# One decoder layer in fp32 on one core: a bias table stored in 16 copies instead of 128, S5 outputs grouped by four state tiles, and two activation tiles at other SBUF offsets

## The chip, the core and the metric

The kernel runs on one core of a Trainium2 chip. The metric is the device time in microseconds of one execution. A core has five engines that run beside each other: TensorE (PE; its weight loads, PEld, overlap its matmuls), VectorE (DVE), ScalarE (ACT), GpSimd (POOL) and SyncE (SP). Each has an instruction stream of its own, run in order; 16 DMA engines serve the transfers that the engines' queues issue. The profile gives TensorE's granted clock as a share: 1.00 is 2.4 GHz, 0.50 is 1.2 GHz.

## The reference

One decoder layer over 256 tokens of width 2048, all in float32: a token mixer, a cross attention into 256 memory tokens and a gated MLP, each followed by a residual and a layer norm. The mixer has three groups behind one input projection: an S5 state space group (512 channels, 32 groups of 16 channels with 64 complex states each), 8 stick-breaking attention heads and 16 NSA heads. What matters here, in the reference's words:

```python
# S5 group: per 16-channel group a diagonal complex recurrence, then the outputs from its states
xr_in = jnp.einsum('btgc,gpc->btgp', ug, br)
xi_in = jnp.einsum('btgc,gpc->btgp', ug, bi)
_, _, sr, si = lax.associative_scan(_complex_affine, (a_r, a_i, xr_in, xi_in), axis=1)
y = jnp.einsum('btgp,gcp->btgc', sr, c_re) - jnp.einsum('btgp,gcp->btgc', si, c_im)
y = y.reshape(bsz, t_len, S5_CH) + d * uf
...
# NSA: a T5 relative-position bias (32 buckets x 16 heads) is added to the logits;
# it depends on the distance t - s of query and key alone
```

## The kernel before

The program walks once through the layer. Every weight matrix comes in chunks of 128x1024 float32 (512 KB). SyncE's queue loads a chunk into `raw` (4 buffers), ScalarE copies it rounded to `hi` (L277, 3 buffers), VectorE subtracts the rest, `lo = raw - hi` (L278, 3 buffers), and TensorE makes three matmuls of every 128x128 piece: hi by hi, hi by lo, lo by hi. Two helpers do this. In `mm3` (L292 to L294) the weights are stationary and the activations move, 256 columns at a time, 24 matmuls a chunk; it serves the mixer's input projection with `A` as moving operand, and the up-projection of the MLP, w_up, with the four tiles `mix` as moving operand (`mix0` and `mix1` for the first half of the contraction, `mix2` and `mix3` for the second). In `mm3x` (L300 to L302) the activations are stationary and the weights move, up to 512 columns at a time; it serves the output projections, among them that of the MLP, w_down, whose activations lie in `A` (re-used) and `act`.

The S5 group runs beside the mixer's projections: `s5_work` is a Python generator from which each weight chunk takes some steps, so its instructions stand between those of the projections. It first builds two tables `Ec` and `Es` [128, 16 state tiles, 256 tokens] (cosines and sines of the rotation), then for each state tile s takes the inputs (two matmuls into `pb`), turns them by the table, scans, and turns back into `s5z`. `outputs(s, ...)` multiplies `s5z` by the matrix `cmat` (in listings `s5c`): two matmuls of 32 columns into column quarter s modulo 4 of a PSUM tile `pa`, the real part and the imaginary one, and after each fourth state tile a VectorE instruction that ends the group. The profile gives these matmuls the line of a small helper, L182, which only orders an S5 instruction behind a projection's. A matmul with float32 operands leaves two records in the trace.

The NSA bias is made by `nsa_bias`, early in the mixer: one small matmul gives `g_sb`, 384 values for each of 16 heads, in 16 SBUF partitions. GpSimd's queue writes it to a DRAM tile `g_dr`, 128 copies of each head's row. In `nsa`, after the queries, ScalarE's queue reads it back into `slab` [128 partitions, 16 heads, 256] through a skewed access pattern with a step of 383 where a copy has 384 values: partition p reads copy p one value further back, which turns the bias by distance into a bias by query and key. Four transfers bring four heads each, 1 KB for each partition and head. VectorE reads `slab` first in L992 and L994 (bias added to a head's logits, and the minimum taken); exponentials, sums and the transposes of L1018 on TensorE follow, head by head. Ahead of them stand the eight tiles of queries, `nq`: ScalarE L940 and VectorE L941 take each from its projection.

The order of the instructions on each engine is fixed when the kernel is built, by a scheduler that simulates the program with priorities by lane; at run time each engine follows it and waits on semaphores. TensorE's stream therefore has projections, S5 matmuls and attention matmuls interleaved as that scheduler put them. Pools decide where tiles lie in SBUF.

Of the kernel before, what the change touches and what calls it, by code (L numbers as in the profile page):

```python
# [8 lines left out]
F32 = mybir.dt.float32  # L9
F32R = mybir.dt.float32r  # L10
ACTF = mybir.ActivationFunctionType
ALU = mybir.AluOpType
# [21 lines left out]
LN2_LO = math.log(2.0) - LN2_HI  # L34
RES_COLS = ((0, 512), (512, 512), (1024, 512), (1536, 256), (1792, 256))
CST_AT = 3
NORM0, NORM1, HOLD = 3, (2,), 2
TABLE_PACE, SCAN_PACE = 0.8, 2.8
BUCKET_FROM = [16, 21, 27, 35, 46, 59, 77, 99, 128, 166, 216]
# [150 lines left out]
class Program:  # L190
    def __init__(self, tc, a, out, ctx):
        self.tc, self.nc, self.a, self.out, self.ctx = tc, tc.nc, a, out, ctx
        pool = lambda name, bufs, **kw: ctx.enter_context(tc.tile_pool(name=name, bufs=bufs, **kw))
        self.lanes = {"first": 0, "split": 100_000, "mixer": 200_000, "proj": 300_000,
                      "late": 400_000}
        self.cur_lane, self.turns = "mixer", False
        self.holds = []
        self.background, self.pace, self.credit = None, 0.0, 0.0
        self.last_hi = self.last_lo = self.last_mm = None
        self.mm_marks = [None, None, None]  # L200
        self.bv = Behind(self, self.nc.vector, lambda: self.last_lo)
        self.bs = Behind(self, self.nc.scalar, lambda: self.last_hi)
        self.bt = Behind(self, self.nc.tensor, lambda: self.mm_marks[-2])
        tc.cur_priority = self.lanes["mixer"]
        self.consts = pool("consts", 1)
        self.wraw = pool("wraw", 4)
        self.whi = pool("whi", 3)
        self.wlo = pool("wlo", 3)
        self.acts = pool("acts", 1)
        self.stat = pool("stat", 2)  # L210
        self.pj = pool("pj", 3, space=bass.MemoryType.PSUM)
        self.op = pool("op", 1, space=bass.MemoryType.PSUM)
        self.mx = pool("mx", 2, space=bass.MemoryType.PSUM)
        self.pq = pool("pq", 1, space=bass.MemoryType.PSUM)
        self.dram = pool("dram", 1, space=bass.MemoryType.DRAM)

    @contextmanager
    def lane(self, name):
# [396 lines left out]
    def s5_work(self, cr, ci, f, fh, fl):  # L615
# [39 lines left out]
                         start=True, stop=True)  # L655
            return bu

        def outputs(s, sr):
            t, rows = s // 4, slice(32 * (s % 4), 32 * (s % 4) + 32)
            if s % 4 == 0:  # L660
                self.yps = self.pq.tile([128, 512], F32, name="pa")
            for i in range(2):
                T.matmul(self.yps[rows, :256], cmat[:, i, s, :], sr[:, i],
                         start=i == 0, stop=i == 1)
            if s % 4 == 3:
                V.scalar_tensor_tensor(self.s5y[:, t, :], u[:, t, :], self.s5d[:, t:t + 1],
                                       self.yps[:, :256], ALU.mult, ALU.add)

        bu, before = inputs(0), None
        yield 1  # L670
        for s in range(16):
            bu2 = bu.rearrange("p (i t) -> p i t", i=2)
# [7 lines left out]
            V.tensor_mul(m2, bu2, sb)  # L680
            if s < 15:
                bu = inputs(s + 1)
            if before is not None:
                outputs(s - 1, before)
            yield 1
            V.tensor_add(z[:, 0], m1[:, 0], m2[:, 1])
            V.tensor_sub(z[:, 1], m1[:, 1], m2[:, 0])
# [5 lines left out]
            V.tensor_mul(m3, z, cb)  # L693
            yield 1
            V.tensor_mul(m4, z, sb)
            before = w.tile([128, 2, 256], F32, name="s5z")
            V.tensor_sub(before[:, 0], m3[:, 0], m4[:, 1])
            V.scalar_tensor_tensor(before[:, 1], m3[:, 1], -1.0, m4[:, 0], ALU.mult, ALU.subtract)
            yield 1
        outputs(15, before)  # L700
        yield 1

    def s5_inputs(self, cr, ci):
# [116 lines left out]
    def nsa_bias(self):  # L820
        nc, a, V, S = self.nc, self.a, self.nc.vector, self.nc.scalar
        both = self.nsq.tile([33, 2, 384], F32, name="oh", tag="kv")
        oh, g_sb = both[:, 0], both[0:NH, 1]
        tab = self.nsq.tile([33, NH], F32, name="tab")
        nc.scalar.dma_start(oh, a["oh"])
        V.memset(tab[32:33, :], -BIG)
        nc.scalar.dma_start(tab[0:32, :], a["relb"])
        g_ps = self.mx.tile([128, 512], F32, name="mx")
        nc.tensor.matmul(g_ps[0:NH, 0:384], tab, oh, start=True, stop=True)
        S.activation(g_sb, g_ps[0:NH, 0:384], ACTF.Copy, scale=-1.0)  # L830

        self.g_dr = self.dram.tile([NH, 128, 384], F32, name="g_dr")
        nc.gpsimd.dma_start(self.g_dr, g_sb.unsqueeze(1).to_broadcast([NH, 128, 384]))

    def nsa_compress(self):
        nc, a, V, S = self.nc, self.a, self.nc.vector, self.nc.scalar
# [109 lines left out]
    def nsa(self):  # L946
# [2 lines left out]
        vcb, vv, gate, ks, q = self.vcb, self.vv, self.gate, self.ks, self.nq  # L949
        g_dr = self.g_dr  # L950
        slab = p.tile([128, NH, 256], F32, name="slab")
        for c in range(4):
            src = bass.AP(g_dr.tensor, g_dr.offset + 127 + c * 4 * 128 * 384,
                          [[383, 128], [128 * 384, 4], [1, 256]])
            nc.scalar.dma_start(slab[:, 4 * c:4 * c + 4, :], src)
        self.after(S.activation(gate, gate, ACTF.Exp, scale=-1.0), self.table)
        V.tensor_scalar(gate, gate, 1.0, None, ALU.add)
        V.reciprocal(gate, gate)
# [285 lines left out]

    def ffn(self, H):
        nc, a, V, S = self.nc, self.a, self.nc.vector, self.nc.scalar
        p = self.ctx.enter_context(self.tc.tile_pool(name="ffp", bufs=1))
        w = self.ctx.enter_context(self.tc.tile_pool(name="ffw", bufs=2))
        cv = p.tile([128, NFF, 2, 4], F32, name="cv")
# [57 lines left out]
```

## Time and profile before

| | |
|---|---|
| device time, median of 3 runs | 1328.58 us (1328.31 to 1328.77) |
| the profiled execution, its own time | 1328.4 us |
| its span, first to last instruction | 1326.6 us |
| mean granted clock of TensorE | 0.989 |
| TensorE busy | 1288.9 us, 97% of the span |
| VectorE, ScalarE busy | 883.9 us (67%), 659.8 us (50%) |
| share of TensorE in the chain that ended last | 89% |

A busy time is the sum of an engine's instructions. The chain is followed back from the last instruction, at each step to what released it, so it tells whose work set the end.

### The profile page before, as it was taken

The page shows a single profiled execution, that of the slowest core. Times are in us where ns is not written, and L with a number is a line of the kernel's source. Part 1 is how long each engine was busy: PE and PEld are TensorE (multiplying, and loading weights), DVE is VectorE, ACT ScalarE, POOL GpSimd, SP SyncE. Part 2 cuts the span into 40 slices and gives each one's busy share as a digit, 9 for nine tenths or more (in the row PEclk, how much of TensorE's full clock was granted, in tenths as well). Part 3 has the DMA queues.
Part 4 walks back from the last instruction along what each step waited for, and adds up shares of the span by engine and source line. Part 5 has one row for each costly group of instructions (what it writes and reads, how often), then busy time and mean ns, then how long its engine had stood idle before and what let it go on. Part 6 is the DMA issues. An engine that isn't in the chain of part 4 may idle for free.

```text
span 1326.6 us, 23002 instructions
## 1 busy us (share of the span) xinstructions
PE 1288.9 (97%) x9221; PEld 1183.9 (89%) x9221; DVE 883.9 (67%) x1510; ACT 659.8 (50%) x1030; POOL 13.8 (1%) x23
## 2 busy tenths in 40 slices
PE   7978999999999999999999999999999999999996
PEld 7767788998779899889999999999999988888896
DVE  7757889787675585766666666666666654544457
ACT  6854333666564346355555555555555543333342
POOL 0200000000000000000000000000000000000000
PEclk9988999999999999989999999999999999999999
DMA  8694335563447555435656555555555665556573
GB/s 305 192 131 162 102 126 155 175 224 111 134 141 256 185 174 199 152 114 191 187 185 188 189 190 191 188 186 187 189 189 190 229 216 188 193 185 193 178 237 129
DMA packets 69414, 240.12 MB, mean 181 GB/s; under 512 B 7723, under 2 KB 10572, under 8 KB 68540
## 3 DMA queue, kind: packets, MB, share of 16 engines
q1 hardware_dynamic: 64720, 230.21, 53.0%
q0 software_dynamic: 1376, 4.98, 2.8%
q10 hardware_dynamic: 3212, 3.47, 0.8%
q8 instruction: 72, 1.18, 0.4%
q14 instruction: 34, 0.28, 0.1%
HBM read 231.82 MB, written 5.24 MB: 179 GB/s over the span
## 4 chain that ended last, share of the span: by engine, by line
PE 89%; DMA 4%; DVE 3%; ACT 2%; issue 1%; POOL 0%; ACTq 0%; DVEq 0%
PE pj L292 17%; PE pj L294 17%; PE pj L293 17%; PE pj L300 10%; PE pj L301 10%; PE pj L302 10%; DMA raw<-in_win_c 2%; PE pa L1025 2%; PE pa L182 1%; DMA s5us<-Ec 1%; DMA raw<-in_win_u 1%; ACT hi L277 1%; PE mx L858 1%; PE mx L988 1%; PE mx L989 1%
## 5 line engine op out<-in xcount | busy, mean ns | idle before, releaser
L278 DVE TENSOR_TENSOR lo<-raw,hi 128x1024 fp32r<-128x1024 f32 (+2 forms) x403 | 488.3, 1212 | 372.9 <-ACT hi L277 369.8
L277 ACT CAST hi<-raw 128x1024 fp32r<-128x1024 f32 (+2 forms) x403 | 419.3, 1040 | 532.5 <-PE pj L293 286.7
L292 PE MATMUL pj<-mix,hi 128*128 128x256 f32 x1472 | 412.4, 281 | 0.8 <-ACT hi L277 0.8
L293 PE MATMUL pj<-mix,hi 128*128 128x256 f32 x1472 | 412.2, 280 | 0.0
L294 PE MATMUL pj<-mix,lo 128*128 128x256 f32 x1472 | 411.4, 280 | 0.0
L292 PEld LDWEIGHTS pj<-mix,hi 128*128 128x128 f32 x1472 | 279.5, 190 | 1.6 <-ACT hi L277 1.3
L293 PEld LDWEIGHTS pj<-mix,hi 128*128 128x128 f32 x1472 | 279.4, 190 | 0.1
L294 PEld LDWEIGHTS pj<-mix,lo 128*128 128x128 f32 x1472 | 279.1, 190 | 0.0
L292 PE MATMUL pj<-A,hi 128*128 128x256 f32 x496 | 144.5, 294 | 16.2 <-ACT hi L277 15.5
L294 PE MATMUL pj<-A,lo 128*128 128x256 f32 x496 | 141.2, 292 | 3.6 <-DVE lo L278 3.6
L293 PE MATMUL pj<-A,hi 128*128 128x256 f32 x496 | 143.0, 291 | 0.0
L292 PEld LDWEIGHTS pj<-A,hi 128*128 128x128 f32 x496 | 97.5, 197 | 21.0 <-ACT hi L277 16.2
L294 PEld LDWEIGHTS pj<-A,lo 128*128 128x128 f32 x496 | 95.6, 196 | 8.5 <-DVE lo L278 4.9
L293 PEld LDWEIGHTS pj<-A,hi 128*128 128x128 f32 x496 | 97.4, 197 | 1.8 <-issue 1.8
L301 PE MATMUL pj<-lo,act 128*128 128x512 f32 (+1 forms) x280 | 97.5, 349 | 0.0
L302 PE MATMUL pj<-hi,act 128*128 128x512 f32 (+1 forms) x280 | 97.5, 349 | 0.0
L301 PE MATMUL pj<-lo,A 128*128 128x512 f32 (+2 forms) x288 | 96.3, 336 | 0.0
L302 PE MATMUL pj<-hi,A 128*128 128x512 f32 (+2 forms) x288 | 96.1, 335 | 0.0
L300 PE MATMUL pj<-hi,A 128*128 128x512 f32 (+2 forms) x288 | 91.5, 335 | 0.0
L300 PE MATMUL pj<-hi,act 128*128 128x512 f32 (+1 forms) x280 | 90.5, 349 | 0.0
L301 PEld LDWEIGHTS pj<-lo,A 128*128 128x128 f32 x288 | 54.5, 189 | 6.7 <-issue 1.0
L302 PEld LDWEIGHTS pj<-hi,A 128*128 128x128 f32 x288 | 54.5, 189 | 5.4 <-issue 0.4
(311 smaller groups left out, 1685.2 us busy)
## 6 DMA issues: line engine op xcount, KB each, us to landing
raw<-in_w_up SPq DMA_DIRECT2D x176, 512.0 KB, 4.3
raw<-in_w_down SPq DMA_DIRECT2D x92, 512.0 KB, 3.4
raw<-in_win_c SPq DMA_DIRECT2D x48, 512.0 KB, 3.8
raw<-in_w_out SPq DMA_DIRECT2D x32, 512.0 KB, 3.4
raw<-in_win_sv SPq DMA_DIRECT2D x8, 512.0 KB, 4.6
raw<-in_wk_m SPq DMA_DIRECT2D x8, 512.0 KB, 4.4
raw<-in_wv_m SPq DMA_DIRECT2D x8, 512.0 KB, 4.4
raw<-in_wq SPq DMA_DIRECT2D x8, 512.0 KB, 4.4
```

The lines of the kernel that those rows point to most:

```text
L182: ins = getattr(self.engine, name)(*args, **kw)
L277: self.last_hi = nc.scalar.copy(hi[:, :n], raw[:, :n])
L278: self.last_lo = nc.vector.tensor_sub(lo[:, :n], raw[:, :n], hi[:, :n].bitcast(F32))
L292: mm(ps, hi, ah, start=start, stop=False)
L293: mm(ps, hi, al, start=False, stop=False)
L294: self.last_mm = mm(ps, lo, ah, start=False, stop=stop)
L300: mm(ps, ah, hi, start=start, stop=False)
L301: mm(ps, ah, lo, start=False, stop=False)
L302: self.last_mm = mm(ps, al, hi, start=False, stop=stop)
L858: mm(h_ps[:, 0:75].rearrange("p (g n) -> p g n", g=5), w1[:, i * 128:i * 128 + 128], kv[:, :, 2 * l:2 * l + 16 * NC_ - 15:16], start=l == ...
L988: mm(zs, q[:, t, gl, qs], kh[:, 0:m], start=True, stop=False)
L1025: ins = mm(o[64 * r:64 * r + 64, gl, 128 * c:256], vv[:, c, v, :], pt[:, k0:k1], start=start[r] is None, stop=False, skip_group_check=True)
```

## The change

Three edits. The bias is stored in `SKEW` = 16 copies (384 KB) instead of 128 (3072 KB), and `slab` is read in eight transfers of 16 partitions and all 16 heads each instead of four of 128 partitions and 4 heads. The turned-back states are written over `Ec[:, s]` and `Es[:, s]` instead of into `s5z`, and `outputs(t)` issues the eight matmuls of a group of four state tiles at one place of the program, the four real parts first, each on its own column quarter, then the four imaginary ones. And three unused tiles are put between others in SBUF.

```diff
@@ class Program, __init__
         self.wlo = pool("wlo", 3)
+        self.gap("a", 192)
         self.acts = pool("acts", 1)
+        self.gap("m", 64)
         self.stat = pool("stat", 2)
...
+    def gap(self, name, size):
+        self.ctx.enter_context(self.tc.tile_pool(name=f"gap_{name}", bufs=1)).tile(
+            [128, size // 4], F32, name=f"gap_{name}")
@@ s5_work
-        def outputs(s, sr):
-            t, rows = s // 4, slice(32 * (s % 4), 32 * (s % 4) + 32)
-            if s % 4 == 0:
-                self.yps = self.pq.tile([128, 512], F32, name="pa")
-            for i in range(2):
-                T.matmul(self.yps[rows, :256], cmat[:, i, s, :], sr[:, i],
-                         start=i == 0, stop=i == 1)
-            if s % 4 == 3:
-                V.scalar_tensor_tensor(self.s5y[:, t, :], u[:, t, :], self.s5d[:, t:t + 1],
-                                       self.yps[:, :256], ALU.mult, ALU.add)
+        def outputs(t):
+            yps = self.pq.tile([128, 512], F32, name="pa")
+            for i, part in enumerate((Ec, Es)):
+                for r in range(4):
+                    T.matmul(yps[32 * r:32 * r + 32, :256], cmat[:, i, 4 * t + r, :],
+                             part[:, 4 * t + r, :], start=i == 0, stop=i == 1)
+            V.scalar_tensor_tensor(self.s5y[:, t, :], u[:, t, :], self.s5d[:, t:t + 1],
+                                   yps[:, :256], ALU.mult, ALU.add)
...
-            if before is not None:
-                outputs(s - 1, before)
+            if s and s % 4 == 0:
+                outputs(s // 4 - 1)
...
-            before = w.tile([128, 2, 256], F32, name="s5z")
-            V.tensor_sub(before[:, 0], m3[:, 0], m4[:, 1])
-            V.scalar_tensor_tensor(before[:, 1], m3[:, 1], -1.0, m4[:, 0], ALU.mult, ALU.subtract)
+            V.tensor_sub(Ec[:, s, :], m3[:, 0], m4[:, 1])
+            V.scalar_tensor_tensor(Es[:, s, :], m3[:, 1], -1.0, m4[:, 0], ALU.mult, ALU.subtract)
@@ nsa_bias
-        self.g_dr = self.dram.tile([NH, 128, 384], F32, name="g_dr")
-        nc.gpsimd.dma_start(self.g_dr, g_sb.unsqueeze(1).to_broadcast([NH, 128, 384]))
+        self.g_dr = self.dram.tile([NH, SKEW, 384], F32, name="g_dr")
+        nc.gpsimd.dma_start(self.g_dr, g_sb.unsqueeze(1).to_broadcast([NH, SKEW, 384]))
@@ nsa
-        for c in range(4):
-            src = bass.AP(g_dr.tensor, g_dr.offset + 127 + c * 4 * 128 * 384,
-                          [[383, 128], [128 * 384, 4], [1, 256]])
-            nc.scalar.dma_start(slab[:, 4 * c:4 * c + 4, :], src)
+        for c in range(128 // SKEW):
+            src = bass.AP(g_dr.tensor, g_dr.offset + 127 - c * SKEW,
+                          [[383, SKEW], [SKEW * 384, NH], [1, 256]])
+            nc.scalar.dma_start(slab[c * SKEW:c * SKEW + SKEW], src)
@@ ffn
+        self.gap("f", 128)
         p = self.ctx.enter_context(self.tc.tile_pool(name="ffp", bufs=1))
```

Where the tiles lie then, as the build places them (byte in a partition, modulo 256): `hi`, `lo`, `raw`, `mix0` and `mix1` at 32 and `mix2`, `mix3` at 224 before and after; `A` at 32 before and 224 after; `act` at 160 before and 32 after. In the changed kernel the lines lie further down: `mm3` is L300 to L302, `mm3x` L308 to L310, `hi` and `lo` L285 and L286, the helper of the S5 matmuls L183, the slab's transfers L962, its first readers L999 and L1001, the queries' two instructions L947 and L948.

How the order of instructions changes is shown at three places. The first is TensorE's stream in the middle of the S5 scan, before: two output matmuls of a state tile (operand `s5z`) between projection matmuls.

```order
L292 MATMUL pj<-A,hi 128x256
L182 MATMUL pa<-s5z,s5c 32x256
L293 MATMUL pj<-A,hi 128x256
L182 MATMUL pa<-s5z,s5c 32x256
L294 MATMUL pj<-A,lo 128x256
```

The same stream after, at two places of a group of four: a real-part matmul (operand `Ec`) alone, and further on the last real-part one with the four imaginary-part ones (operand `Es`).

```order
L302 MATMUL pj<-A,lo 128x256
L300 MATMUL pj<-A,hi 128x256
L183 MATMUL pa<-Ec,s5c 32x256
L301 MATMUL pj<-A,hi 128x256
...
L302 MATMUL pj<-A,lo 128x256
L300 MATMUL pj<-A,hi 128x256
L183 MATMUL pa<-Ec,s5c 32x256
L183 MATMUL pa<-Es,s5c 32x256 x4
L301 MATMUL pj<-A,hi 128x256
```

The scheduler still brings three of the four real-part matmuls forward to where each operand is ready; the fourth and the imaginary parts stand together.

The second place is VectorE's stream at the start of the NSA heads, before: the last queries and one `lo`, then the first reading of `slab`.

```order
L941 SCALAR_TENSOR_TENSOR nq<-pj,nq 64x256 x2
L278 TENSOR_TENSOR lo<-raw,hi 128x1024
L941 SCALAR_TENSOR_TENSOR nq<-pj,nq 64x256
L992 ISA tt,mn<-mx,slab 128x128
L992 ISA mn 128x1
L994 ISA tt,mn<-mx,slab 128x256
```

And after:

```order
L948 SCALAR_TENSOR_TENSOR nq<-pj,nq 64x256 x2
L286 TENSOR_TENSOR lo<-raw,hi 128x1024
L948 SCALAR_TENSOR_TENSOR nq<-pj,nq 64x256
L286 TENSOR_TENSOR lo<-raw,hi 128x1024
L948 SCALAR_TENSOR_TENSOR nq<-pj,nq 64x256 x3
L286 TENSOR_TENSOR lo<-raw,hi 128x1024
L999 ISA tt,mn<-mx,slab 128x128
```

Two more `lo` and three more query instructions stand ahead of the first reading of `slab`.

The third place is ScalarE's stream, which issues the slab's transfers, before:

```order
L940 ACTIVATE nq<-pj 64x256 x2
L955 DMA slab<-g_dr 128x4x256
L277 CAST hi<-raw 128x1024
L955 DMA slab<-g_dr 128x4x256 x3
L940 ACTIVATE nq<-pj 64x256
```

And after:

```order
L947 ACTIVATE nq<-pj 64x256 x2
L962 DMA slab<-g_dr 16x16x256
L285 CAST hi<-raw 128x1024
L962 DMA slab<-g_dr 16x16x256 x4
L947 ACTIVATE nq<-pj 64x256
L962 DMA slab<-g_dr 16x16x256
L285 CAST hi<-raw 128x1024
L947 ACTIVATE nq<-pj 64x256 x2
L962 DMA slab<-g_dr 16x16x256 x2
```

The last three of the eight issues stand behind one more query instruction or three and one more `hi`.

## Rows read from the trace of the kernel before

**Rows 1.** The page: the span, each engine's busy time, and the chain that ended last by engine.

```profile
span 1326.6 us, 23002 instructions
...
PE 1288.9 (97%) x9221; PEld 1183.9 (89%) x9221; DVE 883.9 (67%) x1510; ACT 659.8 (50%) x1030; POOL 13.8 (1%) x23
...
PE 89%; DMA 4%; DVE 3%; ACT 2%; issue 1%; POOL 0%; ACTq 0%; DVEq 0%
```

**Rows 2.** The mixer in five stretches. Columns: start and end, length in us, then busy us (instructions) of TensorE, its weight loads, VectorE, ScalarE and GpSimd, TensorE's granted clock, the busy share of the DMA engines, GB/s.

```profile
60.00:84.00 24.00, 21.09 (x143) 18.76 (x144) 22.82 (x38) 21.52 (x27) 1.04 (x1) 0.93 0.79 114
84.00:112.00 28.00, 18.71 (x99) 15.77 (x97) 12.89 (x21) 8.74 (x13) 0.57 (x1) 0.76 0.89 208
112.00:245.00 133.00, 133.00 (x912) 110.77 (x911) 109.21 (x193) 52.72 (x89) 2.56 (x3) 1.00 0.41 128
245.00:290.00 45.00, 44.30 (x366) 43.73 (x366) 40.49 (x85) 30.36 (x61) 0.00 (x0) 1.00 0.67 217
290.00:415.00 125.00, 125.00 (x820) 102.56 (x820) 88.98 (x311) 75.60 (x196) 0.00 (x0) 1.00 0.43 141
```

**Rows 3.** The waits from 60 to 125 us: who waits for whom, us in sum, how many, the longest.

```profile
ACT hi L277 <- DMA raw<-in_win_c: 17.2, 3, 9.8
PE pj L292 <- ACT hi L277: 9.3, 2, 5.9
```

**Rows 4.** The DMA view of 66 to 102 us: packets, MB and share of the 16 engines' time by queue (q0 is GpSimd's here, q1 SyncE's), then the transfers that were issued there, count, KB each, median us from issue to landing. The last line is the page's, for the whole run.

```profile
q0 software_dynamic: 704, 3.15, 80.8%
q1 hardware_dynamic: 555, 2.01, 13.7%
g_dr<-oh POOLq DMA_DIRECT2D x1, 3072.0 KB, 35.8
raw<-in_win_c SPq DMA_DIRECT2D x6, 512.0 KB, 22.9
...
raw<-in_win_c SPq DMA_DIRECT2D x48, 512.0 KB, 3.8
```

**Rows 5.** Two stretches behind the two holes of TensorE, columns as in rows 2.

```profile
92.40:98.50 6.10, 6.04 (x22) 4.51 (x23) 1.90 (x3) 0.01 (x1) 0.00 (x0) 0.50 1.02 169
103.40:108.80 5.40, 5.33 (x21) 4.72 (x22) 5.35 (x8) 1.97 (x5) 0.00 (x0) 0.50 0.77 272
```

**Rows 6.** From TensorE's timeline: start in us, duration, instruction. First the start and the end of 34 steps in the mixer's projection, with A moving; then in w_up the first matmul on the tiles at 32, the first on the tiles at 224, and the first of the next 24 at 32, 24 matmuls apart each; last the count of one of the three lines with A moving from 112 to 436 us (busy us, mean ns).

```profile
415.81 0.28 PE L293 MATMUL pj<-A,hi 128*128 128x256 f32 x1
...
419.89 0.28 PE L294 MATMUL pj<-A,lo 128*128 128x256 f32 x1
...
701.02 0.28 PE L292 MATMUL pj<-mix,hi 128*128 128x256 f32 x1
...
703.89 0.28 PE L292 MATMUL pj<-mix,hi 128*128 128x256 f32 x1
...
706.62 0.28 PE L292 MATMUL pj<-mix,hi 128*128 128x256 f32 x1
...
L293 PE MATMUL pj<-A,hi 128*128 128x256 f32 x379 | 108.6, 287 | 0.0
```

**Rows 7.** The same in w_down, twelve 512-wide matmuls apart: the start of a chunk with A stationary, of the next with act, of the one after; then the counts of one of the three lines on act and on A over the run.

```profile
1150.13 0.62 PE L300 MATMUL pj<-hi,A 128*128 128x512 f32 x2
...
1152.85 0.64 PE L300 MATMUL pj<-hi,act 128*128 128x512 f32 x2
...
1155.64 0.63 PE L300 MATMUL pj<-hi,act 128*128 128x512 f32 x2
...
L301 PE MATMUL pj<-lo,act 128*128 128x512 f32 x168 | 66.3, 395 | 0.0
L301 PE MATMUL pj<-lo,A 128*128 128x512 f32 x128 | 50.1, 392 | 0.0
```

**Rows 8.** S5 output matmuls: one alone and the instruction behind it, two together and the one behind them; eight matmuls on alternating halves of the columns (L1025) and the one behind; last the count of the S5 outputs' records.

```profile
125.04 0.62 PE L182 MATMUL pa<-s5z,s5c 128*32 128x256 f32 x2
125.59 0.23 PE L798 MATMUL mx<-m,m 128*128 128x128 bf16 x1
...
201.05 1.05 PE L182 MATMUL pa<-s5z,s5c 128*32 128x256 f32 x4
202.03 0.38 PE L301 MATMUL pj<-lo,A 128*128 128x256 f32 x1
...
356.02 0.87 PE L1025 MATMUL pa<-pt,vv 128*64 128x256 f32 x8
356.82 0.39 PE L988 MATMUL mx<-kh,nq 128*128 128x256 f32 x1
...
L182 PE MATMUL pa<-s5z,s5c 128*32 128x256 f32 x64 | 20.1, 405 | 0.0
```

**Rows 9.** The slab: its issues on ScalarE's queue, the DMA view of 276.5 to 287.5 us by queue (q10 is ScalarE's, q1 SyncE's), VectorE's first use, and TensorE's first transpose behind it.

```profile
275.02 0.40 ACTq L955 DMA_DIRECT2D slab<-g_dr  x1
276.91 3.02 ACTq L955 DMA_DIRECT2D slab<-g_dr  x3
...
q10 hardware_dynamic: 2112, 2.10, 57.0%
q1 hardware_dynamic: 485, 1.75, 43.0%
...
280.85 0.29 DVE L992 CUSTOM_DVE_ANT_0 tt<-mx,slab 128x128 f32<-128x128 f32 x1
...
287.87 0.28 PE L1018 MATMUL op<-cst,pe 128*128 128x128 f32 x1
```

More of the change, by code (lines that the diff above doesn't have):

```diff
@@ L36 @@
 CST_AT = 3
+SKEW = 16
 NORM0, NORM1, HOLD = 3, (2,), 2
@@ L656, in inputs @@
             return bu
-        def outputs(s, sr):
-            t, rows = s // 4, slice(32 * (s % 4), 32 * (s % 4) + 32)
-            if s % 4 == 0:
-                self.yps = self.pq.tile([128, 512], F32, name="pa")
-            for i in range(2):
-                T.matmul(self.yps[rows, :256], cmat[:, i, s, :], sr[:, i],
-                         start=i == 0, stop=i == 1)
-            if s % 4 == 3:
-                V.scalar_tensor_tensor(self.s5y[:, t, :], u[:, t, :], self.s5d[:, t:t + 1],
-                                       self.yps[:, :256], ALU.mult, ALU.add)
-        bu, before = inputs(0), None
+        def outputs(t):
[6 more added lines that the diff above has]
+                                   yps[:, :256], ALU.mult, ALU.add)
+        bu = inputs(0)
         yield 1
@@ L695, in s5_work @@
             V.tensor_mul(m4, z, sb)
-            before = w.tile([128, 2, 256], F32, name="s5z")
-            V.tensor_sub(before[:, 0], m3[:, 0], m4[:, 1])
-            V.scalar_tensor_tensor(before[:, 1], m3[:, 1], -1.0, m4[:, 0], ALU.mult, ALU.subtract)
+            V.tensor_sub(Ec[:, s, :], m3[:, 0], m4[:, 1])
+            V.scalar_tensor_tensor(Es[:, s, :], m3[:, 1], -1.0, m4[:, 0], ALU.mult, ALU.subtract)
             yield 1
-        outputs(15, before)
+        outputs(3)
         yield 1
```

## The prediction

> **What bounds the kernel now.** I read the page first, then time by stretches, then the waits, transfers and starts inside the stretches the change touches. The page [rows 1] gives TensorE 97% of the span and 89% of the chain that ended last: what counts is TensorE's own work, plus the places where it stands still. The stretches [rows 2] say where those are. From 112 to 245 us TensorE is busy 133.00 of 133.00 us and VectorE only 109.21; from 290 to 415 it is 125.00 of 125.00 against 88.98. There every nanosecond of matmul is a nanosecond of the run. From 60 to 84 VectorE is the bound (22.82 of 24.00), and nothing in the change touches that. From 84 to 112 neither is: TensorE does 18.71 us of work in 28 and its clock averages 0.76.
>
> The waits [rows 3] explain that last stretch: matmuls waited 9.3 us, two times, for ScalarE's `hi`, and that waited 17.2 us, three times, for the weights' `raw`. The transfers [rows 4] say why. From 66 to 102 us `g_dr` takes 35.8 us to land and 80.8% of all engine time, and a weight load issued then takes 22.9 us to land against 3.8 otherwise. After each of the two holes TensorE works at the lower level, 1.2 GHz: the granted clock is 0.50 for 6.04 and 5.33 us of work [rows 5], which at full clock are half as long, so 5.7 us are lost.
>
> The 16 partitions that `g_dr` is read from set its pace: 3.15 MB in 80.8% of 36 us are 108 GB/s. The old `slab`, into 128 partitions, moved 2.10 MB in 57.0% of 11 us [rows 9], 335 GB/s for the engine time that it had.
>
> **The change part by part, against the profiled 1328.4 us** (the median is 1328.58, the same to 0.02%).
>
> *Bias store, 384 KB for 3072.* At 108 GB/s it takes 3.6 us, and the weights keep up. Both holes and the slow clock go: 9.3 + 5.7 = 15.0 us. VectorE has 12.89 us of work in the 84 to 112 stretch, which would shrink to 13 us: it becomes nearly co-bound there, so something of the 15 comes back as waits for `lo`. In 112 to 245, with TensorE's part shortened as below, VectorE's 109 us stand in about 120, 91%, spread unevenly. I put +2 us on both; the bounds are 0 and 5.7 (the clock's whole part).
>
> *S5 outputs.* Now 64 records [rows 8], 32 matmuls in two passes each, in 24 lone pairs of records and 4 double ones. A lone one delays the next matmul by 0.55 us (125.04 to 125.59), a double one by 0.98 (201.05 to 202.03): 24 × 0.55 + 4 × 0.98 = 17.1 us, and some 0.1 us behind each for refilling, 19.9 together. In the new order three of the four first matmuls of a group stand alone still (their operand is ready early), and the fourth stands with the four of `Es`: 12 × 0.65 + 4 blocks of five. Whether matmuls on different column quarters run beside each other no row shows for this shape; the nearest, eight on two column halves, took 0.80 us for eight (356.02 to 356.82). If the quarters overlap a block costs about 1.1 us, total 12.2, gain 7.7; if not, 2.4 us each (five at half of 0.98), total 17.4, gain 2.5. By the row of the halves I take −7.
>
> *A's new place.* `A` moves from 32 to 224 (bytes modulo 256), away from `hi` and `lo` at 32. The w_up loop has both cases in one tile [rows 6]: the first 24 matmuls, with the `mix` tiles at 32 moving, take 703.89 − 701.02 = 2.87 us, 0.1196 each; the next 24, with those at 224, take 2.73, 0.1138. `A` at 32 goes at 4.08 us for 34 steps, 0.1200. So 6 ns are to be had for each matmul with A moving; there are 379 × 3 = 1137 from 112 to 436 us, all where TensorE is the bound: −6.5 us. Bounds: 0, if the halves differ by something else, and −7.
> The Trainium skill ("TensorE: Matmul & The Clock Gate", Part 2, step ①) says that loading the next weights takes no read bandwidth from the running matmul, as the two have ports of their own. By that rule this term would be 0 and the time 6.5 us more; the two halves of one w_up tile, same shape and weights from the same pools, speak against it.
>
> *act's new place.* In w_down the operands swap roles: twelve 512-wide matmuls with `A` (at 32) stationary take 1152.85 − 1150.13 = 2.72 us, with `act` (at 160) 1155.64 − 1152.85 = 2.79 [rows 7]. `act` comes to 32, `A` goes to 224. 504 such matmuls on act (168 × 3) at 0.0058 us are −2.9; the 384 on A, at an offset that no row has for this role, may lose up to 2.2. I take −2, between −3 and 0.
>
> *The slab.* This speaks against the change. Before, the queue issues it from 275.02 us, all its 2.10 MB move between 276.5 and 287.5, VectorE uses it first at 280.85 and the first transpose that rests on that runs at 287.87 [rows 9]. Now each transfer goes into 16 partitions and carries a slice of all heads, so the first head needs all eight. Say T for the first issue. VectorE's new order has two more `lo` ahead of the slab's first use, 48 matmuls or 5.5 us, so TensorE comes to the first transpose at T + 18.3 (12.85 + 5.5) and the slab must be there at T + 11.3 (7.0 us pass from its first use to that transpose). At `g_dr`'s 108 GB/s 2.10 MB take 19.4 us; with the weights beside it, at the 3.15 MB in 36 us that it really got, 24.0. With 1.5 us from issue to moving it lands between T + 20.9 and T + 25.5: 9.6 to 14.2 us late. I take 12. Nothing else that TensorE could do is ahead of it: the matmuls of the queries are through, and the NSA heads all wait for the slab. With a hole of that length the clock falls as after the two holes above, which cost 5.7 us together: +3 (bounds 0 and 3). Bounds of the stall: 0, if transfers into different groups of 16 partitions run beside each other; 24, if the weights take 43% of the engine time as they did beside the old slab (19.4 / 0.57 = 34.0 us, landing at T + 35.5).
> The Trainium skill ("SBUF — State Buffer", Door 1: The DMA port swizzle) gives the rule: the partitions reached, not the bytes, decide, and partitions 0 to 15 reach 4 of 16 ports, measured there at 104 GB/s. By it the slab takes 20.2 us, an estimate; this trace agrees, with `g_dr`'s 108.
>
> Sum: −15 + 2 − 7 − 6.5 − 2 + 12 + 3 = −13.5, or 1314.9: **1315 us**.
>
> **The rivals.**
> - *The slab comes hidden after all* (eight groups of 16 partitions at once, at the old slab's pace): without its 15 us, 1300 us. For it: the transfers are in one queue, and nothing in the program orders them one behind another. Against: if they do run one behind another, each has only the pace of 16 partitions, as `g_dr` had, and no row shows transfers of one queue spread over different partition groups. 22%.
> - *The offsets give nothing*: 8.5 us less gain, about 1323. For it: all cases compared also differ in what else runs beside them. Against: the halves alternate within one tile. 10%.
> - *Slower: slab and weights turn by turn.* Late by L, the run takes 1328.4 − 28.5 + 3 + L = 1302.9 + L, and is slower by 0.2% when L passes 28.3 us, that is when the slab needs over 38 us, or gets less than half of the engine time (19.4 / 38). If each engine takes one packet of each queue in turn, a 1 KB slab packet at 6.77 GB/s (108 / 16) lasts 0.15 us, and one of the weights' 3.6 KB (1.75 MB in 485, at 43.0% of 11 us × 16) 0.16: share 0.49, 40 us, and 1333. Against: beside the old slab 2112 packets passed in the time of 485 of the weights, and the weights stop when their four `raw` are full. 6%.
> - That the edit of the S5 outputs changes nothing costs 4 us or so: inside the forecast's own range.
>
> **How the numbers follow.** Forecast (the slab waits 8 to 16 us, the other terms near their values) 58%: 1309 to 1320. Slab hidden 22% at 1300 (1297 to 1304); offsets without effect 10% at 1323; slower 6%; about 4% for what I don't see. The range reaches over the hidden slab, since that holds more than 2 in 10, down to 1298 and up to 1325: it takes in the first three cases but for their tails. A run of this kernel can be told from no change at about 0.2%, 2.7 us. Faster by more: 0.91; within: 0.04, the upper end of the stall's bounds (1327); slower: 0.05.
>
> **What would show it.** In the trace after: no wait of a matmul for `hi` between 80 and 110 us, `g_dr` landing in under 6 us, weights near 4 us and the clock at 1.00 there. A-moving matmuls at 0.114 us apart instead of 0.120; w_down's act groups at 2.72 for twelve. L183 beside `Es` in blocks of about 1.1 us. At the NSA start a wait of VectorE's L999 for `slab<-g_dr`, 20 us or more from issue to landing, a hole in TensorE of 8 to 16 us before the first transpose, and 0.50 of clock behind it. I am wrong if the slab lands within 11 us of its first issue, if A's matmuls stay at 0.120, or if the weights starve behind the slab so that a second hole follows.

## The result and the profile after

The changed kernel takes 1310.94 us (median of four, 1309.34 to 1312.0) against 1328.44 for the kernel before: 17.5 us less between these medians, and a ratio of 0.9876, 95% interval 0.9864 to 0.9887, which is 16.5 us. 1315 was forecast, with a range of 1298 to 1325. The profiled execution took 1312.0 us.

The page after, with the lines that answer to [rows 1]:

```profile
span 1310.2 us, 23007 instructions
...
PE 1266.3 (97%) x9221; PEld 1172.5 (89%) x9221; DVE 882.8 (67%) x1510; ACT 659.6 (50%) x1030; POOL 13.3 (1%) x23
...
PE 90%; DMA 3%; DVE 3%; ACT 2%; issue 1%; SPq 0%; ACTq 0%; DVEq 0%
```

The whole gives little away: TensorE has 22.6 us less of busy time and the span is 16.4 us shorter, so something new stands in between. The stretches show where, in the columns of [rows 2]:

```profile
60.00:84.00 24.00, 19.25 (x144) 17.09 (x144) 22.80 (x38) 23.97 (x31) 1.15 (x2) 1.00 0.55 151
84.00:112.00 28.00, 28.00 (x217) 24.37 (x216) 25.99 (x44) 12.59 (x22) 0.00 (x0) 1.00 0.47 153
112.00:245.00 133.00, 132.41 (x1015) 119.67 (x1014) 120.11 (x206) 65.73 (x111) 2.56 (x3) 1.00 0.47 147
245.00:290.00 45.00, 32.13 (x249) 30.80 (x248) 26.64 (x83) 18.84 (x46) 0.00 (x0) 0.85 0.82 165
```

Between 84 and 112 us TensorE now works all 28 us at full clock, 217 matmuls for 99. Between 245 and 290 it works 32 of 45 us, where it worked 44.3. The first is the bias store, the second the slab. The store, by the DMA view of 60 to 110 us (against [rows 4]):

```profile
raw<-in_win_c SPq DMA_DIRECT2D x14, 512.0 KB, 3.6
g_dr<-oh POOLq DMA_DIRECT2D x1, 384.0 KB, 5.7
```

And the slab: TensorE's longest wait from 240 to 430 us, VectorE's idle time ahead of the slab's readers with the transfers' time to land, the DMA view by queue from 248 to 274 us, and the stretches in and behind the hole.

```profile
PE mx L995 <- DVE tcs L1007: 12.5, 1, 12.5
...
L962 ACTq DMA_DIRECT2D slab<-g_dr x8: 328/490/1851, 247.8 to 254.0; - x8
  DMA slab<-g_dr: 14.5, 1
DMA to landing us min/median/max: 6.0/13.3/19.5
...
q10 hardware_dynamic: 2176, 2.10, 72.4%
q1 hardware_dynamic: 711, 2.60, 35.7%
...
262.00:266.00 4.00, 0.32 (x3) 0.11 (x1) 0.00 (x0) 0.00 (x0) 0.00 (x0) 0.92 1.15 119
266.00:270.00 4.00, 0.00 (x0) 0.00 (x0) 0.00 (x0) 0.00 (x0) 0.00 (x0) 0.50 1.14 122
...
274.80:279.00 4.20, 4.18 (x19) 4.20 (x20) 3.73 (x21) 4.13 (x11) 0.00 (x0) 0.50 0.20 41
```

The last transfer is issued at 254.0 and takes 19.5 us, so the slab is there at 273.5, 25.7 us after its first issue at 247.8. TensorE stands for 12.5 us, its clock falls to 1.2 GHz within the hole and stays there for the first 4.2 us of work behind it, which costs another 2.1. ScalarE's queue has 72.4% of the engine time for 2.10 MB.

A run can be laid over another by the start of ScalarE's copy of the n-th weight chunk to `hi`, counted from 0, since all kernels here load the same 403 chunks:

| chunk | before, us | after, us | difference | what lies ahead of it |
|---|---|---|---|---|
| 18 | 61.7 | 62.6 | +0.8 | S5 tables |
| 24 | 98.5 | 83.3 | -15.2 | bias store |
| 69 | 274.0 | 246.6 | -27.4 | S5 scan, A moving |
| 108 | 441.0 | 426.8 | -14.3 | slab, NSA heads, A moving |
| 320 | 1078.6 | 1064.6 | -14.1 | cross attention, w_up |
| 400 | 1302.8 | 1286.5 | -16.2 | w_down |

### The profile page after: what moved, and what is told of

Its sections match the earlier page's. It is cut to its first block, busy times and chain, and to the rows that moved or that the text cites. A ratio compares the mean times of both kernels' runs of the same rounds, so it can differ in the third digit from the quotient of the medians.

```text
span 1310.2 us, 23007 instructions
## 1 busy us (share of the span) xinstructions
PE 1266.3 (97%) x9221; PEld 1172.5 (89%) x9221; DVE 882.8 (67%) x1510; ACT 659.6 (50%) x1030; POOL 13.3 (1%) x23
## 4 chain that ended last, share of the span: by engine, by line
PE 90%; DMA 3%; DVE 3%; ACT 2%; issue 1%; SPq 0%; ACTq 0%; DVEq 0%
PE pj L302 17%; PE pj L300 17%; PE pj L301 17%; PE pj L309 10%; PE pj L308 10%; PE pj L310 10%; PE pa L1032 2%; DMA raw<-in_win_u 2%; DMA slab<-g_dr 1%; PE pa L183 1%; PE mx L995 1%; DVE lo L286 1%; PE mx L996 1%; PE mx L865 1%; ACT hi L285 1%
## 5 line engine op out<-in xcount | busy, mean ns | idle before, releaser
L286 DVE TENSOR_TENSOR lo<-raw,hi 128x1024 fp32r<-128x1024 f32 (+2 forms) x403 | 488.4, 1212 | 350.3 <-ACT hi L285 349.1
L285 ACT CAST hi<-raw 128x1024 fp32r<-128x1024 f32 (+2 forms) x403 | 419.5, 1041 | 517.4 <-PE pj L301 291.2
L300 PE MATMUL pj<-mix,hi 128*128 128x256 f32 x1472 | 412.4, 281 | 0.8 <-ACT hi L285 0.8
L302 PE MATMUL pj<-mix,lo 128*128 128x256 f32 x1472 | 411.7, 280 | 0.0
L300 PEld LDWEIGHTS pj<-mix,hi 128*128 128x128 f32 x1472 | 279.4, 190 | 1.6 <-ACT hi L285 1.3
L302 PEld LDWEIGHTS pj<-mix,lo 128*128 128x128 f32 x1472 | 279.2, 190 | 0.1
L300 PE MATMUL pj<-A,hi 128*128 128x256 f32 x496 | 140.0, 285 | 8.2 <-ACT hi L285 7.2
L302 PE MATMUL pj<-A,lo 128*128 128x256 f32 x496 | 139.1, 287 | 4.7 <-DVE lo L286 4.6
L301 PE MATMUL pj<-A,hi 128*128 128x256 f32 x496 | 138.8, 283 | 0.0
L300 PEld LDWEIGHTS pj<-A,hi 128*128 128x128 f32 x496 | 94.3, 191 | 10.6 <-ACT hi L285 8.1
L302 PEld LDWEIGHTS pj<-A,lo 128*128 128x128 f32 x496 | 93.1, 191 | 9.9 <-DVE lo L286 5.9
L310 PE MATMUL pj<-hi,act 128*128 128x512 f32 (+1 forms) x280 | 96.8, 347 | 0.0
L310 PE MATMUL pj<-hi,A 128*128 128x512 f32 (+2 forms) x288 | 95.6, 333 | 0.0
L301 PEld LDWEIGHTS pj<-A,hi 128*128 128x128 f32 x496 | 94.2, 191 | 0.8 <-issue 0.8
L308 PE MATMUL pj<-hi,A 128*128 128x512 f32 (+2 forms) x288 | 91.0, 334 | 0.0
L308 PE MATMUL pj<-hi,act 128*128 128x512 f32 (+1 forms) x280 | 89.7, 347 | 0.0
L309 PEld LDWEIGHTS pj<-lo,act 128*128 128x128 f32 x280 | 52.9, 189 | 6.6
```

The costliest lines, as they stand in the source:

```text
L285: self.last_hi = nc.scalar.copy(hi[:, :n], raw[:, :n])
L286: self.last_lo = nc.vector.tensor_sub(lo[:, :n], raw[:, :n], hi[:, :n].bitcast(F32))
L300: mm(ps, hi, ah, start=start, stop=False)
L301: mm(ps, hi, al, start=False, stop=False)
L302: self.last_mm = mm(ps, lo, ah, start=False, stop=stop)
L308: mm(ps, ah, hi, start=start, stop=False)
```

## The experiments

Each was timed against the kernel before on the same chip; ratios come with 95% intervals.

**One edit at a time.** Three kernels made from the kernel before, each with one of the edits of the change and nothing of the others.

```diff
bias_only: the edits of nsa_bias and nsa
s5_only:   the edits of s5_work
gaps_only: gap("a", 192), gap("m", 64), gap("f", 128)
```

> The kernel before with the bias edit alone (16 copies, eight slab transfers of 16 partitions). Theory: two large terms of opposite sign, about -15 to -17 us at the store of the bias (no starved weights, full clock between 84 and 110 us) and about +13 us at the slab (hole of some 12 us before the first transposes, half clock behind it): 1324 to 1327 us, same or a little faster. Rival: the slab's hole is there only because the other edits brought TensorE to the heads earlier; then without them it is under 5 us and the run takes about 1316 us.

Measured: 1328.14 us, 1.0003 (0.9994 to 1.0013). At chunk 24 the run is 14.9 us ahead, and TensorE waits at the slab for longer than in the changed kernel:

```profile
PE mx L989 <- DVE tcs L1001: 13.3, 1, 13.3
```

At chunk 108 it is 0.07 us behind. The bias edit as written moves a loss of 15 us from one place to another. The rival falls: the hole does not come from the other edits.

> The kernel before with the S5 edit alone. Theory: column quarters run beside each other, a block of five matmuls takes 0.98 us, and the stretch from 112 to 245 us shortens by 7 to 9 us: about 1320 us. Rival: that stretch also needs VectorE, and the gain there comes back as waits for lo: 1324 us or more.

Measured: 1322.92 us, 0.9966 (0.9955 to 0.9978): 4.5 us gained, where the matmuls alone gave 6.9 (from the start of each output to the next instruction, 18.1 us before and 11.2 here). Three of the four blocks of five do take 0.98 us (at 123.35, 161.21 and 225.45 us); the fourth, at 195.07 with the clock low, takes 1.26. At chunk 36 it is 5.2 us ahead, at chunk 42 1.8. In between TensorE waits for VectorE near 190 us, 1.2 and 0.6 us, and the clock is low behind it. VectorE itself waits just ahead of that; the run bias_undone, below, shows the same hole in more lines.

> The kernel before with the three gaps alone (A at 224, act at 32). Forecast as recorded: -6.5 us in the mixer's projections and -2 us in w_down, 1320 us, A-moving matmuls 0.114 us apart everywhere. Rival, from the changed kernel's trace, where A moves at 0.114 in some stretches and 0.118 in others: -4 and -2 us, about 1322 us, and the same two paces here. A second rival: the faster stretches owe their pace to the S5 edit; then 0.118 everywhere here and about 1324 us.

Measured: 1320.84 us, 0.9948 (0.9933 to 0.9962). Two paces of A-moving matmuls are there, without the S5 edit, so the second rival falls: here from 411.73 to 414.45 us 24 steps of 0.113 (and 0.118 from 241 to 253 us), and in the changed kernel, in the same projection, 24 of 0.1175 from 407.82 to 410.64.

```profile
411.73 0.28 PE L299 MATMUL pj<-A,hi 128*128 128x256 f32 x1
...
414.45 0.28 PE L299 MATMUL pj<-A,hi 128*128 128x256 f32 x1
```

```profile
407.82 0.28 PE L302 MATMUL pj<-A,lo 128*128 128x256 f32 x1
...
410.64 0.28 PE L302 MATMUL pj<-A,lo 128*128 128x256 f32 x1
```

The mean over all A-moving matmuls that follow each other directly is 0.1197 before, 0.1159 after and 0.1155 here: 3.8 to 4.2 ns each, not 6. The run's time came out as forecast all the same, and that is luck: 1.5 us of it were gained between chunks 120 and 160, where the edit touches no term of mine. There the clock stands at 0.50 for 3.4 us (from 565.4) in the profiled execution of this run, and for 6.8 us (from 569.6) in that of the kernel before; 3.4 us less at half the clock are worth 1.7 us. bias_s5, which has no gaps, has the short stretch too, so it is no effect of the offsets.

The three ratios leave 0.03%, -0.34% and -0.52%, together 0.8% or 11 us; the change brought 16. The surplus had to have a place.

**Two edits at a time.** bias_undone is the changed kernel with `nsa_bias` and the slab's reading as before; bias_s5 and bias_gaps add the bias edit to s5_only and gaps_only.

```diff
bias_undone, from the changed kernel:
-        self.g_dr = self.dram.tile([NH, SKEW, 384], F32, name="g_dr")
+        self.g_dr = self.dram.tile([NH, 128, 384], F32, name="g_dr")
...
-        for c in range(128 // SKEW):
+        for c in range(4):
...
```

> The changed kernel with the bias store and the slab as before (128 copies); S5 outputs and gaps stay. Theory: the bias edit moves 15 us from the store to the slab and is worth about nothing beside the other two as well; the other two together are worth more than apart, because the hole of the S5 edit alone near 190 us does not come up with both: about 1311 us. Rival: what is more than the sum of the single edits belongs to the bias edit (TensorE is free of its two early holes and can use what the others give): then this run takes what the two give apart, about 1316 us.

Measured: 1315.75 us, 0.9916 (0.9901 to 0.9931). The rival holds: S5 edit and gaps simply add up, and the surplus of 5 us belongs to the bias edit, which alone is worth nothing. The trace has a hole that the changed kernel has not. VectorE's waits from 176 to 192 us, TensorE's from 112 to 262, and two stretches of 4 us:

```profile
DVE pb L870 <- PE mx L865: 2.2, 1, 2.2
...
PE pb L183 <- DVE s5m L183: 1.2, 1, 1.2
PE pj L300 <- DVE kl L927: 0.6, 1, 0.6
PE pj L309 <- DVE lo L286: 0.6, 1, 0.6
...
188.00:192.00 4.00, 2.19 (x11) 1.97 (x11) 3.91 (x8) 1.78 (x3) 0.00 (x0) 0.78 0.20 56
192.00:196.00 4.00, 4.00 (x29) 3.26 (x29) 3.94 (x7) 1.05 (x1) 0.00 (x0) 0.80 0.62 214
```

VectorE stands 2.2 us at a copy of one column (L870) that needs a matmul of NSA's compression (L865) which TensorE has not reached. Queued behind it are a scan, its products and a `lo`, TensorE then waits 1.8 us for these, and works at a clock of 0.78 and 0.80 for two stretches of 4 us. In the changed kernel the same copy waits 0.25 us and TensorE does not wait. That VectorE waits there is not enough for a hole, though. In the kernel before it waits at the same line for the same matmul, 1.8 and 2.0 us, and TensorE does not stand:

```profile
DVE pb L863 <- PE mx L858: 3.8, 2, 2.0
```

The orders of this run and of the changed kernel differ at some 70 places of VectorE's stream, mostly in where a `lo` stands, and no run moves the copy alone. That its place makes the hole is likely from these lines, but not shown.

> The kernel before with the bias and the S5 edit, without the gaps. The S5 edit alone leaves a hole of 1.8 us near 190 us with slow clock behind it, which the changed kernel does not have. Theory: that hole hangs on the order that the builder gives when the bias store is long; with the short one it goes, and the two edits together are worth about 5 us more than apart: about 1318 us, and no wait of TensorE between 112 and 245 us. Rival: the surplus needs all three edits; then this run is the sum of the two, about 1324 us, with the hole.

Measured: 1317.61 us, 0.9927 (0.9912 to 0.9942). TensorE's only wait from 112 to 250 us:

```profile
PE pj L293 <- DVE kl L920: 0.6, 1, 0.6
```

The hole is gone, and the pair is worth 9.7 us where the sum of the two alone was 4. The theory holds in what it forecast, the time and the missing hole; which change of the order removes the hole is open.

> The kernel before with the bias edit and the gaps, without the S5 edit. Theory (the surplus belongs to bias and S5 edit together): the sum of the two alone, +0.8 and -6.5: about 1321.5 us. Rival (it belongs to bias and gaps, or to all three): 1316 us or less.

Measured: 1322.82 us, 0.9966 (0.9956 to 0.9976). No surplus without the S5 edit. In all eight combinations of the three edits the hole near 190 us is there with the S5 edit and the long bias store, and in no other; the surplus is there with the S5 edit and the short store, and in no other. The hole accounts for only part of the 5 us: between chunks 36 and 42 it costs 3.4 us in s5_only and 2.4 in bias_undone. I have not located the rest.

**The slab's pace.** Two sizes of the same thing, and another way to read it.

```diff
skew32, skew64:
-SKEW = 16
+SKEW = 32            (64)
copies24:
-SKEW = 16
+SKEW = 24
...
-        for c in range(128 // SKEW):
-            src = bass.AP(g_dr.tensor, g_dr.offset + 127 - c * SKEW,
-                          [[383, SKEW], [SKEW * 384, NH], [1, 256]])
-            nc.scalar.dma_start(slab[c * SKEW:c * SKEW + SKEW], src)
+        for h in range(NH):
+            src = bass.AP(g_dr.tensor, g_dr.offset + 127 + h * SKEW * 384,
+                          [[368, 8], [383, 16], [1, 256]])
+            nc.scalar.dma_start(slab[:, h, :], src)
```

> The changed kernel with 32 copies: four slab transfers of 32 partitions, 768 KB of bias. Theory: partitions per transfer set the pace; twice as many land within about 13 us of the first issue instead of 25.7, the hole is 3 us or less, and the run takes 1299 to 1303 us; the bias store at twice the size takes some 8 us and starves nothing. Rival: the order or the packets set it, not the partitions: hole of 12 us still, 1311 us.

> The changed kernel with 64 copies: two slab transfers of 64 partitions, 1536 KB of bias. If pace goes with the number of partitions, the slab lands within 9 us of its first issue. By the Trainium skill (SBUF - State Buffer, Door 1: The DMA port swizzle) partitions 0 to 63 reach no more ports than 0 to 31, so it would be as with 32 copies, some 13 us. The bias store takes some 16 us and may starve weights for a few us of the early stretch: 1299 to 1305 us in all.

Measured: skew32 1305.41 us, 0.984 (0.9824 to 0.9857); skew64 1309.91 us, 0.9872 (0.9857 to 0.9887). The queue of the slab in the DMA views of 248 to 268 us with 32 copies and 251 to 270.5 with 64, then TensorE's wait at the slab in each:

```profile
q10 hardware_dynamic: 2112, 2.10, 50.1%
...
PE mx L995 <- DVE tcs L1007: 7.6, 1, 7.6
```

```profile
q10 hardware_dynamic: 2080, 2.10, 51.7%
...
PE mx L995 <- DVE tcs L1007: 8.9, 1, 8.9
```

From bytes and engine time: 16 partitions a transfer moved 2.10 MB in 72.4% of 26 us, 112 GB/s; 32 in 50.1% of 20 us, 210; 64 in 51.7% of 19.5 us, 208; and 128 in 57.0% of 11 us, 335 [rows 9]. Twice the partitions doubled the pace from 16 to 32 and added nothing from 32 to 64, as the Trainium skill says ("SBUF — State Buffer", Door 1: The DMA port swizzle: partitions 0 to 63 reach no more ports than 0 to 31).

The size of the hole was wrong in both expectations, though: 7.6 us instead of 3. I had taken the pace for the time. With 32 partitions the slab had about half of the engine time, with the weights of the next chunks on the other half (2.58 MB, 46.0%), so 2.10 MB at 210 GB/s took 20 us and not 10. With 64 copies the store lands in 19.0 us and the run is only 8.8 us ahead at chunk 24 instead of 15.2.

> The changed kernel with another slab: 24 copies of the bias, read in sixteen transfers of 128 partitions and one head each (steps 368 and 383, so partition 16c+r reads copy c+r). Theory: 16 partitions a transfer are what made the slab late; with 128 it lands within 10 us of its first issue, the hole of 12.5 us and the half clock behind it go, and the run takes 1297 to 1300 us. Rival: it is the small number of copies, read by many partitions, or the 1 KB packets beside the weights, that is slow; then the hole stays and the run takes about 1311 us. Second rival: the heads are bound by VectorE after the start, and half of the hole comes back there: about 1304 us.

Measured: 1301.63 us, 0.9802 (0.9787 to 0.9816), and TensorE's wait at the start of the heads:

```profile
PE mx L995 <- DVE nq L948: 3.7, 1, 3.7
```

With 24 copies and 128 partitions a transfer, the hole of 12.5 us falls to 3.7 and the run is 9 us faster than the changed kernel, 26 us faster than the kernel before. But the slab does not land within 10 us of its first issue, as the theory had it. VectorE's first reading with its first and last start, the sixteen issues likewise, and the slab's queue from 247 to 267 us:

```profile
L999 DVE CUSTOM_DVE_ANT_0 tt<-mx,slab x32: 259/286/293, 252.6 to 368.2; 128x128 f32<-128x128 f32 x32
...
L962 ACTq DMA_DIRECT2D slab<-g_dr x16: 581/582/689, 247.5 to 263.0; - x16
...
q10 hardware_dynamic: 2112, 2.04, 33.4%
```

Its last packet ends at 267.6 us, 20 us after the first issue, as with 32 copies, and half of its bytes are there at 260.2, as in the changed kernel (260.3). The pace for the engine time used is high, 305 GB/s, but the issues are spread over 15.5 us. VectorE reads the first head at 252.6, when 0.17 of the 2.10 MB have moved: each transfer brings one whole head, where a narrow one brings a slice of all, so the first head need not wait for the last transfer. VectorE's order changes with it: the readings of the first two heads stand ahead of four query instructions that are in front of them in the changed kernel, and the 3.7 us that TensorE still waits are for one of these (`nq`). So the narrow transfers cost in two ways. What their pace costs is about what skew32 gained, 4.9 us of hole; from there to copies24, with the same time to land, it is the whole heads or the new order, and no run separates these two. The rival that few copies are slow to read falls; the time is between the theory and the second rival.

```diff
copies24_pool, from copies24:
-            nc.scalar.dma_start(slab[:, h, :], src)
+            (nc.gpsimd if h % 2 else nc.scalar).dma_start(slab[:, h, :], src)
```

> The kernel copies24 with every second of the sixteen slab transfers issued by GpSimd's queue instead of ScalarE's. Theory: what is left of the slab's cost in copies24 (a wait of 3.7 us of TensorE, ScalarE's exponentials 5.9 us late) is ScalarE issuing sixteen transfers at 0.6 to 0.9 us each ahead of its exponentials; with half of them gone the hole shrinks by 2 to 4 us: 1298 to 1300 us. Rival: the engines' time, shared with the weights, sets it: 1301 us as before. Third: GpSimd's transfers land later than ScalarE's and the heads wait for them: 1305 us.

Measured: 1303.56 us, 0.9822 (0.9807 to 0.9837). TensorE's wait there grew:

```profile
PE mx L995 <- DVE nq L948: 6.7, 1, 6.7
```

Halving what ScalarE issues did not shrink it, so the theory falls. VectorE now waits 3.8 us for a slab transfer, where it waited 0.8 in copies24; GpSimd's eight take 9.4 us to land (median). The third expectation comes nearest; why the two queues together do worse stays open.

**The offsets.** The first halves of the w_up tiles were 6 ns a matmul slower than the second [rows 6], so I moved `mix0` and `mix1` to 224 too.

```diff
mix224, from the changed kernel:
-        self.gap("m", 64)
+        self.gap("m", 256)
...
         self.mix = [None, self.mixp.tile([128, 4, 2, 256], F32R, name="mix1")]
+        self.gap("x", 64)
```

> The changed kernel with the first two mix tiles also moved from 32 to 224 (modulo 256); every tile behind them keeps its offset. Theory: the distance of the moving operand's offset from that of the weights sets the pace of the matmuls: the first halves of the w_up tiles go from 0.120 to 0.114 us apart, 2112 matmuls, -12 us: about 1299 us. Rival: as with A in the last stretches, 0.118: -4 us, 1307 us. Second rival: the halves differ for another reason (what ScalarE and VectorE do in each): no change, 1311 us.

Measured: 1315.64 us, 0.9916 (0.9902 to 0.9931), 4.7 us slower than the changed kernel. All three expectations are wrong in the time; the first rival had the pace of the moved tiles right, 0.118, and missed what the others lost. Two halves in the changed kernel, first on the tiles at 224 and then on those at 32, and two halves here, both at 224:

```profile
700.62 0.29 PE L300 MATMUL pj<-mix,hi 128*128 128x256 f32 x1
...
703.35 0.28 PE L300 MATMUL pj<-mix,hi 128*128 128x256 f32 x1
...
706.22 0.29 PE L300 MATMUL pj<-mix,hi 128*128 128x256 f32 x1
```

```profile
699.76 0.28 PE L300 MATMUL pj<-mix,hi 128*128 128x256 f32 x1
...
702.59 0.28 PE L300 MATMUL pj<-mix,hi 128*128 128x256 f32 x1
...
705.42 0.28 PE L300 MATMUL pj<-mix,hi 128*128 128x256 f32 x1
```

2.73 and 2.87 us for 24 in the one, 2.83 and 2.83 in the other. The tiles at 32 gained 1.7 ns a matmul and those at 224, which had not moved, lost 4: 0.118 throughout. So the offset matters, but not as a pace that belongs to a place.

> The kernel copies24 (1301.6 us) with the four mix tiles, the moving operands of w_up, at four offsets modulo 256: mix0 at 96, mix1 at 160, mix2 at 0, mix3 at 128, everything else in place. If an offset alone set the pace, each tile of 12 matmuls would show its own, steady over the 88 tiles of w_up, and the fastest of them would be the place for all. If the pace is a state that a change of operand tile can start or end, as the last runs suggest (all four at 224: 0.118 throughout; two at 32 and two at 224: 0.120 and 0.113), then tiles change pace some matmuls after the boundary. In time: a pace of 0.113 throughout would be 1290 us, 0.118 throughout 1306 us, 0.120 throughout 1313 us.

Measured: 1309.31 us, 0.9871 (0.9851 to 0.9891), 7.7 us more than copies24. The tiles at 96 go mostly at 0.118; those at 160, 0 and 128 swing between 0.115 and 0.125 from one matmul to the next, with means of 0.118 to 0.119 over w_up. Of the six offsets tried in w_up only 224 was at 0.113 with all its matmuls, and that only next to tiles at 32; `A` at 224 was at it in some stretches, with no tile at 32 moving beside it. What starts or ends the faster pace stays open.

## Why the prediction was right, and where not

The forecast's mechanism holds in the main: the starved weights go, the quarters run beside each other, and the slab comes late. 1310.94 lies 4 us under it, inside its range. Two things were not as it said: `A` moves at the fast pace only in part, and TensorE stands at another place than forecast. Term by term:

- **Bias store, -15 and +2.** -16.0 us between chunks 18 and 24, and `g_dr` lands in 5.7 us. The friction did not come as sized: waits of matmuls for `lo` from 60 to 125 us went from 3.2 to 4.6 us only, and from 112 to 245 us TensorE worked 132.41 of 133 us beside a VectorE at 120.11. This +2 was as much too slow as A's term, below, was too fast, so the two cancel in the sum by luck.
- **S5 outputs, -7.** The quarters do run beside each other: five matmuls, in ten records, take as long as two did, and the records of four quarters begin 7 ns apart. From the start of each output to the next instruction the sum fell from 18.1 to 10.5 us, 0.9 us of it because one output before fell into the slow clock. (There are 26 lone pairs and 3 double ones before, not 24 and 4; the prediction's 17.1 us hardly change by that.) A block after:

```profile
109.39 0.40 PE L183 MATMUL pa<-Ec,s5c 128*32 128x256 f32 x1
109.40 0.42 PE L183 MATMUL pa<-Es,s5c 128*32 128x256 f32 x3
109.63 0.38 PE L183 MATMUL pa<-Ec,s5c 128*32 128x256 f32 x1
109.64 0.80 PE L183 MATMUL pa<-Es,s5c 128*32 128x256 f32 x5
110.37 0.39 PE L301 MATMUL pj<-A,hi 128*128 128x256 f32 x1
```

- **A at 224, -6.5.** Over-sized. 3.8 ns instead of 5.7 a matmul, 1137 of them: -4.3. The row that I read it from was right, and mix224 and gaps_only showed what the reading lacked: 224 has two paces, and in w_up 0.1138 is the pace only between tiles at 32. The forecast's rival of no effect is excluded by the same means, and so is the 0 us that the prediction drew from the Trainium skill ("TensorE: Matmul & The Clock Gate", Part 2, step ①) on separate ports. What makes the pace depend on the offset no run shows.
- **act at 32, -2.** -2.2 us between chunks 320 and 400, and 0.0 there in bias_s5, s5_only and bias_only, which have no gaps. Twelve on `act` take 2.72 us, twelve on `A`, now at 224, 2.74:

```profile
1132.71 0.62 PE L308 MATMUL pj<-hi,A 128*128 128x512 f32 x2
...
1135.45 0.62 PE L308 MATMUL pj<-hi,A 128*128 128x512 f32 x2
...
1138.20 0.61 PE L308 MATMUL pj<-hi,act 128*128 128x512 f32 x2
...
1140.92 0.61 PE L308 MATMUL pj<-hi,act 128*128 128x512 f32 x2
```

- **Slab, +12 and +3.** A hole of 12.5 us and 2.1 us of slow clock. Landing 25.7 us after the first issue T was forecast at 20.9 to 25.5. The place was wrong, though. TensorE does not come to the first transpose at T + 18.3, with the query matmuls through; it stops at T + 14.5, at the logits of the third head (`mx`), which wait until VectorE has read those of the first together with the slab:

```profile
262.04 0.28 PE L301 MATMUL pj<-A,hi 128*128 128x256 f32 x1
274.82 0.55 PE L995 MATMUL mx<-kh,nq 128*128 128x256 f32 x1 [12.50 <-DVE tcs L1007]
```

  The first transpose runs at 281.4 us, T + 33.6, with projection matmuls ahead of it. By the prediction's own count a slab at T + 25.7 is 14.4 us late, so the 12.5 came near its 12 in part by luck. The weights' queue did not starve behind it, and against the turn-by-turn rival's share of 0.49 the slab had 0.72.
- **The hidden slab, 1300 us.** It did not happen in the changed kernel. copies24, with a hole of 3.7 us left, takes 1301.6, so the price was about right, but not by the rival's way: there too the slab is 20 us in coming.

What the prediction did not see is that its sum stands on one order of instructions. The terms are not those of the edits apart: the bias edit alone gives nothing, the S5 edit alone 4.5 us, and they give 9.7 together, with the hole near 190 us gone. The prediction had no row that could have told whether the changed kernel's order has such a hole; that it has none is luck. The expectation for the S5 edit alone, 1320 us, did miss it.

## What to carry to other kernels

The same bytes can come later when each transfer goes to fewer partitions: price a transfer by the partitions of each one and by its share of engine time beside the weights, then look at whether the first reader needs one transfer or all of them. Two positive steps (368 and 383 here) spread a skewed read of 24 copies over 128 partitions, one head a transfer, and kept the saving at the store with most of the hole at the slab gone. Sum terms on the order that will really be built: a single edit tried alone may come with another order of instructions and be worth half of what it is worth beside another edit (4.5 us alone, some 10 beside the bias edit).

## What was not expected of the hardware

Matmuls with a moving operand at 224 and weights at 32 (bytes modulo 256) have two paces with the same operands, 0.113 and 0.118 us, each steady for many microseconds: in w_up 0.1138 where tiles at 32, at 0.120, alternate with them, and 0.118 where all are at 224. And the clock of an idle TensorE falls while it stands: work stops at 262.3 us, the mean from 262 to 266 is 0.92 and from 266 on 0.50, so a hole of 12.5 us cost no more slow time (4.2 us) than the one of 6 us at the store had (6.04 us, [rows 5]).
